# Low parts of all weight blocks on VectorE, fewer background steps in the feed-forward loops, and a later spectrum scaling

## The chip, the cores and the metric

The kernel runs on one core of a Trainium2 chip. The metric is the device time of one execution in microseconds (us); the median of three runs stands for a kernel. A profiled execution has a trace, whose span begins and ends with the first and last instruction that it records; its own time is a little longer than the span.

## The reference

Two layers of a diffusion backbone work on 256 latent tokens and 256 context tokens of 1024 features, in fp32. Each layer is a feed-forward, a token mixer, and a second feed-forward. Every sub-layer is modulated by shift, scale and gate vectors (adaLN) that come from `c` for the latent tokens and from `c_ctx` for the context, and is closed by a layer norm:

```python
def _ffn_sublayer(x, shift, scale, gate, w_in, w_out, g, b):
    a, u = jnp.split(_modulate(x, shift, scale) @ w_in, 2, axis=-1)   # 1024 -> 2 x 2816
    y = (jax.nn.silu(a) * u) @ w_out                                  # 2816 -> 1024
    return _post_ln(x, 0.5 * gate * y, g, b)                          # LN(alpha*x + ...)
...
for i in range(2):
    m  = silu(c) @ mod_w[i] + mod_b[i]        # 9 vectors of 1024 for the latent tokens
    mc = silu(c_ctx) @ mod_w[i] + mod_b[i]    # 9 for the context
    x  = _ffn_sublayer(x, m[0], m[1], m[2], ...);  xc = the same with mc
    h  = _modulate(x, m[3], m[4]);                 hc = the same with mc
    y  = even mixer (Fourier + Hyena long convolution) for i = 0
         odd mixer (two-way GLA + HGRN2 scans, the latent from the context's state) for i = 1
    x  = _post_ln(x, m[5] * y, ...)
    x  = _ffn_sublayer(x, m[6], m[7], m[8], ...)
```

The even mixer runs on both streams; in layer 1 the context is needed only as far as its scan states. The Hyena convolution multiplies spectra; its filters `k` come from a small network of the positions and are divided by the sum of their absolute values, `k / (sum |k| + 1e-6)`.

## The kernel before, in words

**Precision.** Every fp32 product is made of three (`mm3`, lines 463 to 465): an operand is cast to a high part (fp32r) and the rest is its low part; the products are high by high, high by low and low by high. Weights are split on the chip. `Stream` (line 39) holds the list of weight blocks (128 x 1024, 512 KB) in the order in which they are used. SP issues a block's load into one of three `raw` buffers; ScalarE casts it to `whi` (line 78); the low part `wlo` (or `lo`, for a block in spare buffers) is the difference of `raw` and `whi` (line 79), on GpSimd if the block's flag `pool` is set when it is queued, otherwise on VectorE. `whi` and `wlo` have three buffers each. `get()` hands a block out, splits the two after it and loads two further ones.

The flags come from the code that queues the blocks. In a feed-forward the input blocks alternate: the block for `pa` has its low part on VectorE, that for `pu` on GpSimd (`au == 1`). Of the output blocks most with an odd number go to GpSimd. In the mixers a table of numbers (`G0`) decides. In all, 164 low parts are made on GpSimd; 20 or 21 in each of the three feed-forward loops of both streams, 20 to 23 in each of their closes, the others in the mixers, their output products, the head and the last feed-forward.

**The feed-forward.** `ffn` (line 590) makes the hidden features. The first two of the 22 blocks of 128 come from a head in another layout; then 20 turns follow, f from 2 to 21. A turn has two units of 24 matmuls, into `pa` and `pu`. After each unit it advances a queue of background work, `bg`, by a step or two (`step`, line 166): one step after `pa`, two after `pu`. Then ScalarE takes the silu of `pa` (line 616), VectorE multiplies it by `pu` (line 617), ScalarE casts the result to `hh` (line 226) and GpSimd makes its low part (line 227). `hh` lies in 31 buffers of tag `s` that other stages use too, two blocks f per buffer and stream.

`ffn_close` (line 623) has two products of 22 units, of 12 matmuls each, `y <- whi, hh`: the first for the two latent tiles of tokens, the second for the two context tiles. In the first, `fill` advances `bg` by a step at every odd k; then `flush` runs what is left. In the second, the layer norms of the latent tiles are in `bg` and are advanced between the units. Layer norm works on VectorE for the most part (lines 331 to 353), with ScalarE, and GpSimd for the power (line 234).

**Background work.** `mod_vec` (line 238) makes an adaLN vector: for each of 8 blocks of `mod_w` (512 KB, loaded by SP into an `s` buffer) VectorE multiplies it by `c` and by `c_ctx` and sums along the row (line 243, two instructions `mt` of 128 x 1024 per block and step); then one step for the column (line 247), and for gates one with a transpose. In the first loop two generators advance together, so that a step has a part of each: `spectrum` (line 728) for the second Hyena filter, and the adaLN vectors 2 to 7 of layer 0. The second loop has five adaLN vectors, the third four.

`spectrum` takes the filter through: `lin` on TensorE, window and sums on VectorE and GpSimd, `norm1` (the sum of absolute values, in the bank `pn`), the reciprocal `rc` of it (lines 799, 800), diagonal blocks `eb` (line 803), then `scale()`: eight small matmuls `pr <- rc, eb` (line 758) that bring the reciprocal to all rows, and a copy by ScalarE to `rs`, by which the products `pk` are multiplied. A `yield` ends a step. The first filter's spectrum (`early`) runs in the head, whose order is a string written by hand.

**Order.** Each engine runs its instructions in the order in which the program issues them. There is no scheduler: where `step` is called fixes what stands ahead of what on VectorE, GpSimd, ScalarE, TensorE and in SP's queue of loads.

Of the kernel before, what the change touches and what calls it, by code (L numbers as in the profile page):

```python
# [9 lines left out]
F32 = mybir.dt.float32  # L10
# [4 lines left out]
ALU = mybir.AluOpType  # L15
# [23 lines left out]
class Stream:  # L39
# [26 lines left out]
    def split_to(self, i):  # L66
        while self.n_split <= min(i, len(self.units) - 1):
            j = self.n_split
            self.load_to(j + self.ahead_load)
            src, split, spare, pool = self.units[j]  # L70
            if split:
                w = self.raw.pop(j)
                if spare:
                    hi, lo = self.spare([P, 1024], F32R, "hi"), self.spare([P, 1024], F32R, "lo")
                else:
                    hi = self.pool.tile([P, 1024], F32R, tag="whi", name=f"whi{j}")
                    lo = self.pool.tile([P, 1024], F32R, tag="wlo", name=f"wlo{j}")
                self.nc.scalar.copy(hi, w)  # L78
                (self.nc.gpsimd if pool else self.nc.vector).tensor_tensor(lo, w, hi.bitcast(F32), op=ALU.subtract)  # L79
                self.split[j] = (hi, lo)  # L80
            self.n_split += 1

# [20 lines left out]
def g_(n, d):  # L103
    SEEN[n] = G0.get(n, d)
    return G.get(n, G0.get(n, d))
# [23 lines left out]
def kernel(ctx: ExitStack, tc: tile.TileContext, a, out, stop=None):  # L129
# [14 lines left out]
    def S(shape, dt=F32, name="s"):  # L144
        count[0] += 1
        return sp.tile(shape, dt, tag="s", name=f"{name}{count[0]}")

    def H(shape, dt=F32, name="h"):
        count[0] += 1
        return tp.tile(shape, dt, tag="h", name=f"{name}{count[0]}", bufs=5)  # L150
# [5 lines left out]
    def PS(name="ps"):  # L156
        count[0] += 1
        return ps.tile([P, 512], F32, tag="ps", name=f"{name}{count[0]}")
# [7 lines left out]
    def step(n=1):  # L166
        for _ in range(n):
            while bg:
                try:
                    next(bg[0])  # L170
                    break
                except StopIteration:
                    bg.pop(0)

    def flush():
        while bg:
            step()

    def run(*gens):
        for g in gens:  # L180
            for _ in g:
                pass
# [5 lines left out]
    def chain(*gens):  # L188
        for g in gens:
            yield from g  # L190
# [11 lines left out]
    def alternate(*gens):  # L202
        gens = list(gens)
        while gens:
            g = gens.pop(0)
            try:
                next(g)
                gens.append(g)
                yield
            except StopIteration:  # L210
                pass
# [13 lines left out]
    def split(dst_hi, dst_lo, src, lo_eng=None):  # L225
        act.copy(dst_hi, src)  # L226
        (lo_eng or dve).tensor_tensor(dst_lo, src, dst_hi.bitcast(F32), op=ALU.subtract)  # L227
# [62 lines left out]
    def load_ln(ln, l, n, gate, streams=2):  # L290

        ln.append(bcast(a["ln_g"][l, n:n + 1, :], "lng"))
        yield
        ln.append(bcast(a["ln_b"][l, n:n + 1, :], "lnb"))
        ln.append([])
        for s in range(streams):
            yield
            ln[2].append(bcast(gate_d[gate, s:s + 1, :], "gate"))
        yield
# [141 lines left out]
    def close(t, y, gate, g, b, ax, eps, nxt, late=False, fine=False):  # L441


        yield from post_ln(t, y, gate, g, b, ax, eps, fine)
        if nxt is None:
            return
        xn = {}
        yield from norm(t, xn)
        if "all" not in hT:
            new_hT()  # L450
        tr = zipped(to_hT(t, 0, xn[t], *nxt), to_hT(t, 1, xn[t], *nxt))
        if late:
            pend[t] = tr
        else:
            yield from tr
# [6 lines left out]
    def mm3(o, wh, wl, xh, xl, start, stop):  # L462
        pe.matmul(o, lhsT=wh, rhs=xh, start=start, stop=False)  # L463
        pe.matmul(o, lhsT=wh, rhs=xl, start=False, stop=False)  # L464
        pe.matmul(o, lhsT=wl, rhs=xh, start=False, stop=stop)  # L465

    def fm_unit(o, view=lambda x: x):

        hi, lo = ws.get()
        for k in range(KD):  # L470
            mm3(o, hi[:, P * k:P * k + P], lo[:, P * k:P * k + P], view(hT[k][:, 0, :]), view(hT[k][:, 1, :]), k == 0, k == KD - 1)
# [94 lines left out]
    def to_features(dst, pairs, h):  # L566

        yield
        pt = PS("pt")
        for f in range(2 * len(pairs)):  # L570
            pe.transpose(pt[:, P * f:P * f + P], h[:, P * f:P * f + P], ident)
        yield
        for n, b in enumerate(pairs):
            split(b[:, :, 0, dst], b[:, :, 1, dst], pt[:, 256 * n:256 * n + 256].rearrange("p (k t) -> p k t", k=2))
        yield
# [14 lines left out]
    def ffn(l, i, extra=(), head=None):  # L590
        hs = [{0: S([P, 2, 2, L], F32R, name="hh")} for s in range(2)]

        def done(t, y):
            h = H([P, 256], name="ht")
            act.activation(h, y[:, 0:256], AF.Silu)
            dve.tensor_tensor(h, h, y[:, 256:512], op=ALU.mult)
            return to_features(slice(P * (t % 2), P * (t % 2) + P), [hs[t // 2][0]], h)

        todo = (head or tm_head)(range(NT), done)
        bg.extend(extra)  # L600
        for f in range(2, KF):
            if f % 2 == 0:
                for s in range(2):
                    hs[s][f // 2] = S([P, 2, 2, L], F32R, name="hh")
            if f == 5 and stop == "head":
                return hs
            pa, pu = PS("pa"), PS("pu")
            fm_unit(pa)
            if todo:
                run(todo)  # L610
                todo = None
            step(1)
            fm_unit(pu)
            step(2)
            sa = H([P, T], name="sa")
            act.activation(sa, pa, AF.Silu)
            dve.tensor_tensor(sa, sa, pu, op=ALU.mult)  # L617
            for s in range(2):
                h = hs[s][f // 2][:, f % 2]
                split(h[:, 0], h[:, 1], sa[:, L * s:L * s + L], gp)  # L620
        return hs

    def ffn_close(l, i, hs, nxt):


        ln = []
        loads = load_ln(ln, l, 2 * i, GATE_ROW[l, 8 if i else 2])

        def lhs(k, t):
            h = hs[t // 2][k // 2][:, k % 2]  # L630
            c = slice(P * (t % 2), P * (t % 2) + P)
            return h[:, 0, c], h[:, 1, c]

        def fill(k):
            if k % 2:
                step(1)
            if k in range(10, 18, 2):
                next(loads)

        def closing(t, y, late=False):  # L640
            g, b, gates = ln
            return close(t, y, gates[t // 2], g, b, 2 * ALPHA, 4 * EPS, nxt, late, not late)

        y = tok_out(lhs, KF, (0, 1), fill)
        flush()
        hT.clear()
        k0 = key[0] = f"c{l}{i}"
        bg.append(alternate(closing(0, y[0]), closing(1, y[1])))

        def done(t, y):  # L650
            if t == 3:
                hs.clear()
            ws.split_spare(ws.pos + g_(f"{k0}a{t}", 2 * t - 3))
            if t == 3:
                flush()
            bg.append(closing(t, y, True))
            now.append(t)

        def fill(k):
            if now:  # L660
                step(g_(f"{k0}s3", 1))
            elif k >= KF - TAIL:
                step(g_(f"{k0}s2", 1))
            else:
                if k >= KF - TAIL - 3:
                    ws.split_spare(ws.pos + g_(f"{k0}b{KF - TAIL - k}", 1))
                step(g_(f"{k0}s1", 2) if k > g_(f"{k0}s0", 2) else 1)

        now = []
        tok_out(lhs, KF, (2, 3), fill, TAIL, done)  # L670


# [55 lines left out]
    def spectrum(o, hd, w3, win, cs, skip, T=None):  # L728
# [21 lines left out]
        def product(c, e):  # L750
            pk = PS("pk")
            mm3(pk, cs[:, c, 0, e], cs[:, c, 1, e], sd[e][0][:, c], sd[e][1][:, c], True, True)
            return pk
# [53 lines left out]
        if early:  # L807
            for n in todo[:2]:
                pks[n] = product(*n)
                yield  # L810
        rs = scale()
        yield
# [969 lines left out]
    hs = ffn(0, 0, [zipped(chain(spectrum(1, hd, con["w3"], con["win"], cs, lambda: con["skip"]), combine_first()), mods([(0, m) for m in range(2, 8)]))], head)  # L1782
# [14 lines left out]
    hs = ffn(0, 1, [mods([(0, 8)] + [(1, m) for m in range(4)])])  # L1797
# [4 lines left out]
    hs = ffn(1, 0, [mods([(1, m) for m in range(4, 8)])])  # L1802
# [113 lines left out]
```

## Time and profile before

| | us |
|---|---|
| median of 3 runs (1893.0 to 1899.78) | 1894.14 |
| profiled execution, its own time | 1893.39 |
| its span | 1891.6 |
| TensorE (PE) busy | 1761.0 |
| VectorE (DVE) busy | 1259.5 |
| ScalarE (ACT) busy | 724.8 |
| GpSimd (POOL) busy | 721.6 |

Windows of the span, from the trace: the head to 67 us, the loop of the first feed-forward to 321.4, its close to 449.8, the even mixer's products and transforms from 480.4 to 618, the second feed-forward's loop from 686.6 to 914.8, the third's from 1073.4 to 1298, the odd mixer from 1429.3 to 1648.3, the last feed-forward from 1713. Engines are named PE, PEld (weight loads of TensorE), DVE, ACT, POOL and SP in the rows; L79 is line 79. A tile's name is the one that the program gives it. "PEclk" is the clock of TensorE that was granted, as a share of 2.4 GHz.

### The profile page before, as it was taken

Reading aid. Unit: us, or ns where it says so; the run is one execution under the profiler, and the core shown is the slowest. Engines: PE = TensorE matmul, PEld = TensorE weight load, DVE = VectorE, ACT = ScalarE, POOL = GpSimd, SP = SyncE. Lnnn points to the kernel's source line nnn. Section 1 sums busy time; section 2 is a strip of 40 time slices with the busy share of each in tenths; the row PEclk is TensorE's granted clock in tenths of the full one; section 3 lists DMA queues with packets and bytes.
Section 4 is the critical chain, followed back from the end, with each engine's and each line's share of the span. In section 5 each row is a group of like instructions: output and inputs, shape, how many; then the busy total and the mean of one; then the engine's idle time right before and its main releaser. Section 6 shows DMA issues by size and latency. Waiting matters only on the chain. (4 is left out here: it accounts for less than half of the span.)

```text
span 1891.6 us, 22049 instructions
## 1 busy us (share of the span) xinstructions
PE 1761.0 (93%) x8236; PEld 1425.5 (75%) x8236; DVE 1259.5 (67%) x1674; ACT 724.8 (38%) x1070; POOL 721.6 (38%) x467
## 2 busy tenths in 40 slices
PE   6989999998987999999999999999988999879998
PEld 5767778876866778777887787788867778757887
DVE  6688887267599768885247688812377484676755
ACT  5422233344434342223334422323354463443443
POOL 2445434453356223333445233334454353341000
PEclk9989999999998999999999999999999999889999
DMA  8536654644313145553464455433644223335563
GB/s 317 214 132 240 227 189 166 238 167 150 112 45 123 65 164 202 208 203 130 154 233 177 150 213 199 162 110 138 232 166 145 83 91 90 134 131 201 206 215 137
DMA packets 91499, 314.91 MB, mean 166 GB/s; under 512 B 10848, under 2 KB 11584, under 8 KB 91392
## 3 DMA queue, kind: packets, MB, share of 16 engines
q1 hardware_dynamic: 85952, 297.09, 44.0%
q0 software_dynamic: 4576, 15.91, 2.6%
q8 instruction: 64, 1.05, 0.2%
q10 hardware_dynamic: 864, 0.51, 0.1%
q14 instruction: 43, 0.35, 0.1%
HBM read 308.18 MB, written 4.24 MB: 165 GB/s over the span
## 5 line engine op out<-in xcount | busy, mean ns | idle before, releaser
L79 DVE TENSOR_TENSOR wlo<-raw,whi 128x1024 fp32r<-128x1024 f32 x195 | 261.5, 1343 | 330.7 <-ACT whi L78 328.9
L79 POOL TENSOR_TENSOR wlo<-raw,whi 128x1024 fp32r<-128x1024 f32 x137 | 345.9, 2525 | 316.9 <-ACT whi L78 278.4
L78 ACT CAST whi<-raw 128x1024 fp32r<-128x1024 f32 x332 | 343.8, 1050 | 264.9 <-PE y L465 151.9
L243 DVE SCALAR_TENSOR_TENSOR mt<-mraw,cb 128x1024 bf16<-128x1024 f32 x256 | 395.8, 1599 | 11.2 <-DMA mraw<-in_mod_w_dram 8.3
L465 PE MATMUL pu<-hT,wlo 128*128 128x512 f32 x576 | 225.7, 392 | 4.7 <-DVE wlo L79 4.7
L463 PE MATMUL pu<-hT,whi 128*128 128x512 f32 x576 | 225.8, 392 | 0.0
L464 PE MATMUL pu<-hT,whi 128*128 128x512 f32 x576 | 225.4, 391 | 0.0
L227 POOL TENSOR_TENSOR hh<-sa,hh 128x256 fp32r<-128x256 f32 x120 | 87.1, 747 | 344.6 <-ACT hh L226 344.6
L465 PE MATMUL pa<-hT,wlo 128*128 128x512 f32 x480 | 191.3, 398 | 12.0 <-DVE wlo L79 12.0
L463 PE MATMUL pa<-hT,whi 128*128 128x512 f32 x480 | 191.5, 399 | 8.8 <-ACT whi L78 8.7
L464 PE MATMUL y<-wlo,hh 128*128 128x512 f32 x468 | 183.2, 391 | 6.8 <-DVE wlo L79 6.1
L464 PE MATMUL pa<-hT,whi 128*128 128x512 f32 x480 | 189.1, 394 | 0.0
L463 PE MATMUL y<-whi,hh 128*128 128x512 f32 x468 | 182.9, 391 | 0.2 <-ACT whi L78 0.2
L465 PE MATMUL y<-whi,hh 128*128 128x512 f32 x468 | 182.2, 389 | 0.0
L226 ACT CAST hh<-sa 128x256 fp32r<-128x256 f32 x120 | 42.8, 404 | 294.7 <-DVE sa L617 294.7
L465 PEld LDWEIGHTS pu<-hT,wlo 128*128 128x128 f32 x576 | 108.8, 189 | 28.3 <-DVE wlo L79 5.6
L463 PEld LDWEIGHTS pu<-hT,whi 128*128 128x128 f32 x576 | 109.0, 189 | 23.6 <-ACT hh L226 0.8
L464 PEld LDWEIGHTS pu<-hT,whi 128*128 128x128 f32 x576 | 108.9, 189 | 22.6
L465 PEld LDWEIGHTS pa<-hT,wlo 128*128 128x128 f32 x480 | 91.3, 190 | 39.7 <-DVE wlo L79 21.1
L463 PEld LDWEIGHTS pa<-hT,whi 128*128 128x128 f32 x480 | 91.4, 190 | 34.3 <-ACT whi L78 15.7
L464 PEld LDWEIGHTS y<-wlo,hh 128*128 128x128 f32 x468 | 87.8, 188 | 28.6 <-DVE wlo L79 8.4
L464 PEld LDWEIGHTS pa<-hT,whi 128*128 128x128 f32 x480 | 91.4, 190 | 18.7
(419 smaller groups left out, 3272.2 us busy)
## 6 DMA issues: line engine op xcount, KB each, us to landing
raw<-in_ffn_out_dram SPq DMA_DIRECT2D x154, 512.0 KB, 3.4
mraw<-in_mod_w_dram SPq DMA_DIRECT2D x144, 512.0 KB, 5.9
raw<-in_ffn_in_dram SPq DMA_DIRECT2D x120, 512.0 KB, 3.8
raw<-in_ffn_tm_dram SPq DMA_DIRECT2D x44, 512.0 KB, 3.3
raw<-in_od_fm_dram SPq DMA_DIRECT2D x17, 512.0 KB, 3.2
raw<-in_od_tm_dram SPq DMA_DIRECT2D x16, 512.0 KB, 3.3
raw<-in_ffn_head_dram SPq DMA_DIRECT2D x12, 512.0 KB, 4.4
raw<-in_ev_in_dram SPq DMA_DIRECT2D x12, 512.0 KB, 3.5
```

The source lines that it names most:

```text
L78: self.nc.scalar.copy(hi, w)
L79: (self.nc.gpsimd if pool else self.nc.vector).tensor_tensor(lo, w, hi.bitcast(F32), op=ALU.subtract)
L226: act.copy(dst_hi, src)
L227: (lo_eng or dve).tensor_tensor(dst_lo, src, dst_hi.bitcast(F32), op=ALU.subtract)
L243: dve.scalar_tensor_tensor(H([P, D], BF16, "mt"), w, 1.0, cb[s], op0=ALU.mult, op1=ALU.mult, accum_out=acc[:, s, b:b + 1])
L463: pe.matmul(o, lhsT=wh, rhs=xh, start=start, stop=False)
L464: pe.matmul(o, lhsT=wh, rhs=xl, start=False, stop=False)
L465: pe.matmul(o, lhsT=wl, rhs=xh, start=False, stop=stop)
```

## The change

Four edits. Line 79 makes every low part on VectorE, so that the flags are no longer read. A turn of a feed-forward loop has one or two steps after `pu` (one for an even f), not always two: 50 steps in a loop, not 60. In the close, at an odd k, the buffers of `hh` that the product has passed are given up one by one (`hs[0]` in the first product, `hs[1]` in the second), not all at the end. The `spectrum` of the second filter has three more yields between `eb` and `scale()`.

```diff
@@ split_to
                 self.nc.scalar.copy(hi, w)
-                (self.nc.gpsimd if pool else self.nc.vector).tensor_tensor(lo, w, hi.bitcast(F32), op=ALU.subtract)
+                self.nc.vector.tensor_tensor(lo, w, hi.bitcast(F32), op=ALU.subtract)
                 self.split[j] = (hi, lo)
@@ ffn
             step(1)
             fm_unit(pu)
-            step(2)
+            step(1 + f % 2)
             sa = H([P, T], name="sa")
@@ ffn_close, first product
         def fill(k):
             if k % 2:
+                hs[0].pop(k // 2)
                 step(1)
@@ ffn_close, second product
             else:
+                if k % 2:
+                    hs[1].pop(k // 2)
                 if k >= KF - TAIL - 3:
@@ spectrum
                 pks[n] = product(*n)
                 yield
+        else:
+            for _ in range(3):
+                yield
         rs = scale()
         yield
```

VectorE's queue in the first loop, before, around the reciprocal; `wlo` is a low part for a `pa` block, `gc` a column of adaLN, `sa` the gated features of a turn:

```order
L617 TENSOR_TENSOR sa_1071<-sa_1071,pu_981 128x512
L79 TENSOR_TENSOR wlo_1083<-raw_982,whi_1082 128x1024
L247 SCALAR_TENSOR_TENSOR gc_1127<-acc_849,modb 128x16
L799 TENSOR_SCALAR rc_1159<-pn_1110 128x128
L800 RECIPROCAL rc_1159<-rc_1159 128x128
L803 TENSOR_SCALAR eb_1162<-ones,ident 128x128 x4
L243 SCALAR_TENSOR_TENSOR mt_1170,acc_1167<-mraw_1059,cb_809 128x1024
L243 SCALAR_TENSOR_TENSOR mt_1172,acc_1167<-mraw_1059,cb_811 128x1024
L243 SCALAR_TENSOR_TENSOR mt_1183,acc_1167<-mraw_1065,cb_809 128x1024
L243 SCALAR_TENSOR_TENSOR mt_1185,acc_1167<-mraw_1065,cb_811 128x1024
L617 TENSOR_TENSOR sa_1187<-sa_1187,pu_1079 128x512
```

The same place after (lines of `spectrum` have moved by three):

```order
L617 TENSOR_TENSOR sa_1159<-sa_1159,pu_1061 128x512
L79 TENSOR_TENSOR wlo_1173<-raw_1062,whi_1172 128x1024
L802 TENSOR_SCALAR rc_1200<-pn_1140 128x128
L803 RECIPROCAL rc_1200<-rc_1200 128x128
L806 TENSOR_SCALAR eb_1203<-ones,ident 128x128 x4
L243 SCALAR_TENSOR_TENSOR mt_1211,acc_1208<-mraw_1098,cb_809 128x1024
L243 SCALAR_TENSOR_TENSOR mt_1213,acc_1208<-mraw_1098,cb_811 128x1024
L79 TENSOR_TENSOR wlo_1218<-raw_1104,whi_1217 128x1024
L243 SCALAR_TENSOR_TENSOR mt_1247,acc_1208<-mraw_1134,cb_809 128x1024
L243 SCALAR_TENSOR_TENSOR mt_1249,acc_1208<-mraw_1134,cb_811 128x1024
L617 TENSOR_TENSOR sa_1251<-sa_1251,pu_1169 128x512
```

A second low part, that of the `pu` block, now stands among the products of the turn.

ScalarE's queue before, around the copy of the scaling to `rs`:

```order
L616 ACTIVATE sa_1071<-pa_980 128x512
L226 CAST hh_978<-sa_1071 128x256
L226 CAST hh_979<-sa_1071 128x256
L78 CAST whi_1082<-raw_982 128x1024
L78 CAST whi_1131<-raw_1023 128x1024
L760 COPY rs_1179<-pr_1174 128x512
L616 ACTIVATE sa_1187<-pa_1078 128x512
```

And after:

```order
L616 ACTIVATE sa_1251<-pa_1168 128x512
L226 CAST hh_1166<-sa_1251 128x256
L226 CAST hh_1167<-sa_1251 128x256
L78 CAST whi_1262<-raw_1170 128x1024
L78 CAST whi_1298<-raw_1215 128x1024
L763 COPY rs_1337<-pr_1332 128x512
L616 ACTIVATE sa_1345<-pa_1258 128x512
```

Before, `rs` is copied ahead of the silu `sa_1187`, whose gating stands last in VectorE's piece before, so in the turn in which `rc` and `eb` are made. After, that turn's silu is `sa_1251`, and the copy comes ahead of the next one's, `sa_1345`: a turn later.

VectorE in the second product of the first close before, among the layer norms of two tiles (`z`, `x`), where `wlo` is a block's low part:

```order
L342 BN_AGGR mv_3141<-st_3036 128x2
L233 TENSOR_SCALAR rp_3144<-mv_3141 128x1
L79 TENSOR_TENSOR wlo_3150<-raw_3100,whi_3149 128x1024
L342 BN_AGGR mv_3165<-st_3057 128x2
L233 TENSOR_SCALAR rp_3168<-mv_3165 128x1
L347 SCALAR_TENSOR_TENSOR z_3035<-z_3035,mv_3141,lng_2807 128x1024
L347 SCALAR_TENSOR_TENSOR z_3056<-z_3056,mv_3165,lng_2807 128x1024
L353 SCALAR_TENSOR_TENSOR x_3171<-z_3035,rstd_3143,lnb_2845 128x1024
L79 TENSOR_TENSOR wlo_3197<-raw_3147,whi_3196 128x1024
```

And after:

```order
L342 BN_AGGR mv_3141<-st_3036 128x2
L233 TENSOR_SCALAR rp_3144<-mv_3141 128x1
L79 TENSOR_TENSOR wlo_3150<-raw_3100,whi_3149 128x1024
L342 BN_AGGR mv_3165<-st_3057 128x2
L233 TENSOR_SCALAR rp_3168<-mv_3165 128x1
L347 SCALAR_TENSOR_TENSOR z_3035<-z_3035,mv_3141,lng_2802 128x1024
L79 TENSOR_TENSOR wlo_3176<-raw_3121,whi_3175 128x1024
L347 SCALAR_TENSOR_TENSOR z_3056<-z_3056,mv_3165,lng_2802 128x1024
L353 SCALAR_TENSOR_TENSOR x_3171<-z_3035,rstd_3143,lnb_2844 128x1024
L79 TENSOR_TENSOR wlo_3197<-raw_3147,whi_3196 128x1024
```

The low part `wlo_3176`, which was on GpSimd, stands between the two `z` of line 347.

## Rows read from the trace of the kernel before

**Rows 1.** Busy time, share of the span and instructions of each engine:
```profile
PE 1761.0 (93%) x8236; PEld 1425.5 (75%) x8236; DVE 1259.5 (67%) x1674; ACT 724.8 (38%) x1070; POOL 721.6 (38%) x467
```
**Rows 2.** Windows: us, busy (count) of PE, PEld, DVE, ACT, POOL; PEclk, DMA share, GB/s:
```profile
67.00:321.40 254.40, 236.63 (x1027) 188.19 (x1025) 209.67 (x259) 71.06 (x113) 109.99 (x77) 0.97 0.54 197
119.50:129.50 10.00, 5.77 (x18) 4.91 (x19) 9.90 (x17) 1.40 (x4) 2.49 (x1) 0.50 0.74 259
686.60:914.80 228.20, 221.88 (x967) 179.60 (x966) 163.68 (x206) 65.22 (x104) 79.79 (x60) 1.00 0.51 188
1073.40:1298.00 224.60, 220.37 (x964) 179.73 (x963) 138.98 (x173) 65.82 (x103) 76.99 (x59) 1.00 0.48 174
1232.70:1298.00 65.30, 65.30 (x289) 54.05 (x288) 11.97 (x12) 19.27 (x30) 22.99 (x18) 1.00 0.30 104
480.40:618.00 137.60, 121.12 (x561) 98.81 (x561) 116.90 (x149) 57.27 (x91) 71.47 (x39) 0.94 0.28 94
...
1624.50:1641.60 17.10, 15.48 (x63) 13.24 (x64) 7.96 (x14) 2.42 (x4) 0.77 (x1) 0.50 0.28 92
```
**Rows 3.** Groups by line: busy us, mean ns of one, idle before and its releaser:
```profile
L79 DVE TENSOR_TENSOR wlo<-raw,whi 128x1024 fp32r<-128x1024 f32 x195 | 261.5, 1343 | 330.7 <-ACT whi L78 328.9
L79 POOL TENSOR_TENSOR wlo<-raw,whi 128x1024 fp32r<-128x1024 f32 x137 | 345.9, 2525 | 316.9 <-ACT whi L78 278.4
...
L243 DVE SCALAR_TENSOR_TENSOR mt<-mraw,cb 128x1024 bf16<-128x1024 f32 x256 | 395.8, 1599 | 11.2 <-DMA mraw<-in_mod_w_dram 8.3
L465 PE MATMUL pu<-hT,wlo 128*128 128x512 f32 x576 | 225.7, 392 | 4.7 <-DVE wlo L79 4.7
...
L227 POOL TENSOR_TENSOR hh<-sa,hh 128x256 fp32r<-128x256 f32 x120 | 87.1, 747 | 344.6 <-ACT hh L226 344.6
...
L465 PE MATMUL pa<-hT,wlo 128*128 128x512 f32 x480 | 191.3, 398 | 12.0 <-DVE wlo L79 12.0
...
L464 PE MATMUL y<-wlo,hh 128*128 128x512 f32 x468 | 183.2, 391 | 6.8 <-DVE wlo L79 6.1
```
**Rows 4.** Single lines: count, then duration ns min/median/max, first and last start us:
```profile
L243 DVE SCALAR_TENSOR_TENSOR mt<-mraw,cb x256: 1207/1216/3421, 79.6 to 1788.0; 128x1024 bf16<-128x1024 f32 x128
...
L79 DVE TENSOR_TENSOR wlo<-raw,whi x195: 1193/1226/3409, 60.2 to 1872.7; 128x1024 fp32r<-128x1024 f32 x195
...
L79 POOL TENSOR_TENSOR lo<-raw,hi x27: 2340/2418/3381, 22.8 to 1692.6; 128x1024 fp32r<-128x1024 f32 x27
...
L353 DVE SCALAR_TENSOR_TENSOR x<-z,rstd,lnb x9: 1272/3402/3427, 403.9 to 1430.6; 128x1024 f32<-128x1024 f32 x9
```
**Rows 5.** Timeline, one turn of the second loop: start us, us, instruction, [idle before]:
```profile
739.14 1.32 DVE L79 TENSOR_TENSOR wlo<-raw,whi 128x1024 fp32r<-128x1024 f32 x1 [1.73 <-ACT whi L78]
740.20 2.52 POOL L79 TENSOR_TENSOR wlo<-raw,whi 128x1024 fp32r<-128x1024 f32 x1 [0.81 <-POOL hh L227]
740.38 3.42 DVE L243 SCALAR_TENSOR_TENSOR mt<-mraw,cb 128x1024 bf16<-128x1024 f32 x1
...
743.73 1.22 DVE L243 SCALAR_TENSOR_TENSOR mt<-mraw,cb 128x1024 bf16<-128x1024 f32 x1
...
749.46 0.68 DVE L617 TENSOR_TENSOR sa<-sa,pu 128x512 f32<-128x512 f32 x1
...
751.87 1.30 DVE L79 TENSOR_TENSOR wlo<-raw,whi 128x1024 fp32r<-128x1024 f32 x1 [1.74 <-ACT whi L78]
```
**Rows 6.** Timeline, TensorE at the scaling in the first loop:
```profile
123.73 2.08 PE L758 MATMUL pr<-rc,eb 128*128 128x128 f32 x8 [7.59 <-DVE eb L803]
```
**Rows 7.** Timeline, three waits of TensorE in and after the mixers:
```profile
1438.50 1.75 PE L411 MATMUL ptr<-ident,xn 128*128 128x128 f32 x7 [6.15 <-ACT xn L398]
...
1615.83 6.44 DVE L1419 SCALAR_TENSOR_TENSOR OH<-OH,rr,gn 128x128 f32<-128x128 f32 x8
...
1626.12 0.77 PE L1351 MATMUL po<-vg,am 128*128 128x128 f32 x2 [4.45 <-DVE am L1345]
...
1738.41 0.79 PE L464 MATMUL ya<-wlo,hT 128*128 128x512 f32 x1 [3.21 <-DVE wlo L79]
```

## What I expect of the change, and why

> **What bounds the kernel now.** I began with the busy shares [rows 1]: TensorE works for 1761.0 of 1891.6 us, so all that an edit can give back is TensorE's idle time, 130.6 us, and the time in which its clock is low. VectorE (1259.5) and GpSimd (721.6) bound nothing on average. Next I cut the span into windows by stage [rows 2]. A piece of the last feed-forward without a waiting matmul gives the free pitch: 288 matmuls in 65.30 us, 0.2267 each, so a unit of 24 takes 5.44 us and a loop of 20 turns (40 units) 217.6 us. The three feed-forward loops take 254.4, 228.2 and 224.6 us; what stands above 217.6 is 36.8, 10.6 and 7.0, and of the first 36.8 some 10 belong to the extra matmuls of the filter spectrum (1027 against 967). In the even mixer VectorE is busy for 116.9 of 137.6 us; it is the one stage where that engine is close to being the limit.
>
> Then the groups by cost [rows 3] show who holds TensorE up: in the loops the matmuls of `pa` and `pu` waited 12.0 + 4.7 us for low parts, in the second products `y` waited 6.1 us for them. All of these were made on VectorE. Why VectorE is late is in the spread of single durations [rows 4]: the product of an adaLN step (line 243) takes 1.216 us as median and up to 3.421; a low part on VectorE 1.226 and up to 3.409; line 353 has 1.272 at best and 3.402 as median. One turn of a loop shows the cause [rows 5]: GpSimd's low part runs from 740.20 to 742.72, and the VectorE product issued at 740.38 ends only at 743.80. By itself it takes 1.22; it stood still until GpSimd was done. So the 2.4 us low parts on GpSimd are paid for on VectorE.
>
> The Trainium skill, "SBUF — State Buffer", section "Who interferes with whom", says that a VectorE instruction with two SBUF operands and a GpSimd instruction that reads SBUF share a port under an exclusive lock, where the loser stands still and isn't merely slowed. The trace agrees (1.22 became 3.42 behind a GpSimd instruction of 2.52); by that rule the stretch goes with the subtractions, and of the large groups on GpSimd only the 0.747 us instructions of line 227 [rows 3] remain to cause some.
>
> **What the edits do to VectorE's load.** 164 subtractions (137 + 27) leave GpSimd [rows 3, 4]. On VectorE they are worth 164 x 1.226 = 201 us. What comes back: line 243, 256 x (1.599 - 1.216) = 98; its own low parts, 195 x (1.343 - 1.226) = 23; line 353, up to 9 x 2.1 = 19; smaller groups add some. So VectorE's busy total grows by 30 to 60 us, to about 1300 (69%), while its single instructions become 1.2 us long throughout. GpSimd falls by 137 x 2.525 + 27 x 2.418 = 411 to about 310 us.
>
> **The loops.** A turn now takes VectorE from 739.14 to 751.87 = 12.73 us, more than TensorE's two units (10.88), so TensorE waits [rows 5]. In it are a wait of 1.73 for the next high part, one low part, a first product of 3.35 start to start, five more at 1.146 (743.73 to 749.46), and the gating product of 0.68. After: wait 1.73, two low parts at 1.2, the gating product, and one or two adaLN steps between them, so four or six products of 1.15 (a step is two; three steps before, two or three now). That is 1.73 + 2.4 + 0.6 + 4.6 or 6.9 = 9.3 or 11.6, 10.5 as mean against 10.88. The odd turns run over by 0.7 and the even ones give it back; low parts are asked for two units ahead. So TensorE should hardly wait. The second loop then gains most of its 10.6: I take 7. The third, with 7.0 above the pitch, I take at 5. Bounds: 0 and 17.6 for the two.
>
> In the first loop one wait stands alone: the scaling matmuls `pr` wait 7.59 us for `eb` at 123.73 [rows 6], and the clock in 119.5 to 129.5 is granted at 0.50 [rows 2], the lower level (1.2 GHz), which costs 10 x 0.5 = 5 more. With three more yields the matmuls stand behind the next turn's `pu` unit, some 11 us after `eb` is issued, and VectorE has no longer an 11 us stretch ahead of it without a break, so the whole 12.7 should go. The rest of the first loop: PE idle there is 254.4 - 236.63 = 17.8, less 7.6 for `pr` leaves 10.2; the mean clock of 0.97 means about 7.6 lost, less 5 leaves 2.6. Of these 12.8 I take 11, because spectrum work still falls on VectorE between low parts. First loop: 24. Bounds: 0 (if the `eb` wait only moves) and 26.
>
> **The closes.** The second products gain the 6.1 us of `y` [rows 3]: the low parts that waited lose their stretch. Against that, 20 to 23 low parts per close now lie in VectorE's order among layer-norm work, and where that work exceeds TensorE's 12 x 0.2267 = 2.72 us per unit, TensorE must live from the two units split ahead (5.44 us). I take the 6.1 as won. The first loop has 50 steps now, not 60, and its six vectors need 48 for their blocks and some for columns and gates; six blocks are left for the first product of its close: per block 2 x 1.15 us on VectorE, which has little to do there, and a 512 KB load on SP's queue among the product's own. The product streams 0.524 MB per 2.72 us, 193 GB/s; six blocks in 22 units add 53. The 246 stay under the 259 that [rows 2] shows in a window at a share of 0.74, so the loads should fit; I charge 1, with bounds 0 and 4. The tiles given back one by one only let such loads start earlier; that is in the same charge. Net 5; bounds -12 and 6, the lower from 3 closes x 3.8 us, if an excess of half a microsecond in each of seven units per close isn't covered by the two units ahead.
>
> **The other places.** Low parts of mixers and heads: 40 or so of the 164 (20 to 21 in each loop, 20 to 23 in each close). Three waits there hang on a stretched instruction [rows 7]. At 1615.83 eight small products take 6.44 us beside a GpSimd low part, `am` is late, and TensorE waits 4.45 at 1626.12: all of it. `ya` at 1738.41 waits 3.21 for a low part: all of it. `ptr` at 1438.50 waits 6.15 at the end of a chain that has line 353 at 1430.6 in it: 3.4 - 1.27 = 2.1. Together 10. After 1626 the clock is at 0.50 for 17.1 us [rows 2], a loss of 8.5 behind that 4.45 wait; I count half, 4, since I can't tell that this wait alone brought it down. For the even mixer I charge 2: five low parts more on VectorE are 5 x 1.22 = 6.1 of loss in the stage where it is busiest, against up to five stretches of 2.2 that go, 11.
>
> The Trainium skill, "Perfetto Trace Analysis", section "Optimizing Scalar/DVE Operations", advises to move work away from VectorE, to ScalarE or even GpSimd, where VectorE is saturated, with the warning that the shared port may undo it. By the advice the even mixer should lose the 6.1; by the warning it should gain. The trace has both sides there, and only the run can tell.
>
> **The sum.** 24 + 7 + 5 + 5 + 10 + 4 - 2 = 53. The profiled execution took 1893.4 us (1.8 outside its span): 1893.4 - 53 = 1840. The median of the runs is 0.7 above it, which is less than the rounding here.
>
> **Rivals.**
> B, the loops alone gain. In closes and mixers the in-order VectorE queue loses with the added low parts what its shorter instructions win. Gains: 24 + 7 + 5 = 36, less 3 x 3 in the closes and nothing in the mixers: 27, so 1866. For it: `y` already waits for VectorE, not GpSimd, low parts. Against it: those very waits are stretched.
> C, slower: VectorE's queue becomes the bound outside the loops. A low part that GpSimd made beside everything else now stands behind whatever VectorE has ahead of it. If each of the 40 in mixers and heads is exposed for its 1.22 (49 us), the closes lose 3 x 3.8 = 11.4, and the loops gain only the `pr` stall and half the rest (12.7 + 12 = 25), the result is 1893.4 + 49 + 11.4 - 25 = 1929; half of the exposure gives 1904. It decides once VectorE is busy in a mixer for nearly all of its window; the even mixer, at 85%, is the only one close. Against it: TensorE, ScalarE and the chains leave gaps in the odd mixer's VectorE work.
> D, the subtraction isn't what stretches. If the stretch belonged to other GpSimd work (line 227, 120 x 0.747), the load would grow by 201 and only the `pr` stall would go: 1893.4 - 12.7 = 1880, or worse. Against it: 3.42 fits 2.52 + 1.22 less the overlap, and line 227 is too short for that.
>
> **Chances.** Forecast 0.68 (own range 1822 to 1858), B 0.18 (1858 to 1872), D 0.07, C 0.07. Runs of this kernel can't tell less than about 0.5%, 9.5 us, from no change: faster means under 1884.7, which the forecast, B and half of D give, 0.89; same 0.05, from the rest of D and the weakest of C; slower 0.06. The range 1820 to 1870 holds the forecast's own and most of B.
>
> **What would show it.** Right: line 243's median and mean both near 1.22 with a maximum near 2.0; VectorE near 1300 us busy, GpSimd near 310; no `pr` wait above 1 us and clock 1.0 around 120 us; second and third loop at 218 to 222 us; `pa` and `pu` waits for low parts under 5 us in all; the `am` wait gone. Wrong: `y` waiting over 10 us for `wlo` in the second products (B), waits for `wlo`, `lo` or mixer tiles of VectorE in the even mixer beyond those of before with that window above 140 us (C), or line 243 still reaching 3.4 (D).

## The result, and the profile after

The changed kernel takes 1831.66 us (median of 4 runs, 1826.96 to 1833.66) against 1895.55 (4 runs): a ratio of 0.9657, 95% interval 0.9629 to 0.9685. The forecast was 1840, range 1820 to 1870, so the direction and the size were right. Some of the terms behind them were not: the scaling edit won nothing, the loops gained more than the most that was allowed for the first, and the clock's 4 us didn't come, as the runs below show.

Busy time of each engine after, in the columns of [rows 1]:

```profile
PE 1746.5 (95%) x8236; PEld 1425.9 (78%) x8236; DVE 1277.3 (70%) x1838; ACT 725.4 (40%) x1070; POOL 307.5 (17%) x303
```

VectorE took over 164 instructions and is busy only 18 us longer, and GpSimd lost 414 us. The reason stands in the spread of single durations (count, then ns min/median/max), which answer to [rows 4], and in the groups that answer to [rows 3]:

```profile
L243 DVE SCALAR_TENSOR_TENSOR mt<-mraw,cb x256: 1208/1217/2312, 77.1 to 1728.4; 128x1024 bf16<-128x1024 f32 x128
...
L353 DVE SCALAR_TENSOR_TENSOR x<-z,rstd,lnb x9: 1278/1282/2396, 378.0 to 1385.2; 128x1024 f32<-128x1024 f32 x9
```

```profile
L79 DVE TENSOR_TENSOR wlo<-raw,whi 128x1024 fp32r<-128x1024 f32 x332 | 420.5, 1270 | 319.4 <-ACT whi L78 319.0
...
L243 DVE SCALAR_TENSOR_TENSOR mt<-mraw,cb 128x1024 bf16<-128x1024 f32 x256 | 309.8, 1251 | 2.1 <-DMA mraw<-in_mod_w_dram 2.1
...
L464 PE MATMUL y<-wlo,hh 128*128 128x512 f32 x468 | 183.5, 392 | 3.0 <-DVE wlo L79 3.0
```

The adaLN product's mean went from 1.599 to 1.251 us, its longest from 3.421 to 2.312; line 353's median from 3.402 to 1.282. No wait of a matmul of `pa` is left.

The windows after, columns of [rows 2]: the first loop, its close, the even mixer, the second and third loop, the odd mixer, each from the same matmul as before:

```profile
67.40:293.10 225.70, 225.70 (x1027) 184.97 (x1026) 181.46 (x252) 71.42 (x114) 56.04 (x54) 1.00 0.58 208
293.10:420.80 127.70, 124.18 (x546) 100.13 (x545) 94.58 (x124) 56.41 (x65) 10.72 (x12) 1.00 0.66 222
453.90:594.00 140.10, 123.05 (x561) 100.48 (x560) 122.00 (x154) 56.95 (x91) 58.59 (x34) 0.93 0.29 96
661.30:879.60 218.30, 218.30 (x966) 180.51 (x966) 154.50 (x226) 65.82 (x104) 28.35 (x40) 1.00 0.54 195
1038.40:1256.40 218.00, 218.00 (x965) 180.35 (x964) 137.33 (x193) 66.36 (x103) 27.84 (x39) 1.00 0.50 178
1384.70:1595.90 211.20, 201.23 (x1088) 169.50 (x1087) 134.07 (x218) 103.50 (x174) 53.06 (x39) 0.95 0.35 112
```

In all three loops TensorE's busy time is the window: it never waits, and the clock is at 1.00. They give 28.7, 9.9 and 6.6 us (45.2 of the 59.7 by which the span fell). The closes give 4.3, the odd mixer 7.7, what follows it 7.3 (its output product 2.7, the head and body of the last feed-forward 1.3 and 3.3), the head of the second feed-forward 1.5. The even mixer loses 2.6 and the stretches ahead of the mixers and loops some 4.

Where the time went, by stage, in us between the same matmuls of each kernel (e1 to e4 are the first four experiments):

| stage | before | after | e1 low parts | e2 scaling | e3 steps | e4 low parts + steps |
|---|---|---|---|---|---|---|
| first loop | 254.4 | 225.7 | 236.4 | 252.1 | 235.6 | 225.7 |
| its close | 128.4 | 127.7 | 127.0 | 128.2 | 132.4 | 128.0 |
| even mixer | 137.5 | 140.1 | 139.9 | 138.4 | 138.2 | 140.1 |
| second loop | 228.2 | 218.3 | 218.3 | 228.2 | 218.3 | 218.3 |
| third loop | 224.6 | 218.0 | 218.0 | 224.6 | 218.0 | 218.0 |
| third close | 131.3 | 128.3 | 127.8 | 131.1 | 131.5 | 127.8 |
| odd mixer | 219.0 | 211.2 | 209.8 | 216.6 | 218.3 | 211.0 |
| median of runs | 1894.7 | 1831.7 | 1840.3 | 1895.3 | 1867.0 | 1830.7 |

(The median in the column before is that of the runs beside e1 to e4; the one in the column after is that of the result above.)

### The profile page after: what moved, and what is told of

Its sections match the earlier page's. It is cut to its first block, busy times and chain, and to the rows that moved or that the text cites. A ratio compares the mean times of both kernels' runs of the same rounds, so it can differ in the third digit from the quotient of the medians.

```text
span 1831.9 us, 22048 instructions
## 1 busy us (share of the span) xinstructions
PE 1746.5 (95%) x8236; PEld 1425.9 (78%) x8236; DVE 1277.3 (70%) x1838; ACT 725.4 (40%) x1070; POOL 307.5 (17%) x303
## 5 line engine op out<-in xcount | busy, mean ns | idle before, releaser
L79 DVE TENSOR_TENSOR wlo<-raw,whi 128x1024 fp32r<-128x1024 f32 x332 | 420.5, 1270 | 319.4 <-ACT whi L78 319.0
L243 DVE SCALAR_TENSOR_TENSOR mt<-mraw,cb 128x1024 bf16<-128x1024 f32 x256 | 309.8, 1251 | 2.1 <-DMA mraw<-in_mod_w_dram 2.1
L463 PE MATMUL pa<-hT,whi 128*128 128x512 f32 x480 | 187.6, 391 | 0.0
L465 PE MATMUL pa<-hT,wlo 128*128 128x512 f32 x480 | 186.8, 389 | 0.0
L464 PE MATMUL pa<-hT,whi 128*128 128x512 f32 x480 | 186.8, 389 | 0.0
L234 POOL TENSOR_TENSOR rstd<-rp,mhalf 128x1 f32<-128x1 f32 x42 | 35.4, 847 | 483.9 <-DVE rp L233 481.0
```

The source lines that it names most:

```text
L79: self.nc.vector.tensor_tensor(lo, w, hi.bitcast(F32), op=ALU.subtract)
L234: gp.tensor_tensor(dst, t, mhalf.to_broadcast([P, n]), op=ALU.pow)
L243: dve.scalar_tensor_tensor(H([P, D], BF16, "mt"), w, 1.0, cb[s], op0=ALU.mult, op1=ALU.mult, accum_out=acc[:, s, b:b + 1])
```

## The experiments

**One edit at a time.** The first two edits each by itself, on the kernel before.

e1, the low parts alone:

```diff
-                (self.nc.gpsimd if pool else self.nc.vector).tensor_tensor(lo, w, hi.bitcast(F32), op=ALU.subtract)
+                self.nc.vector.tensor_tensor(lo, w, hi.bitcast(F32), op=ALU.subtract)
```

Expected:

> The kernel before with the one edit of line 79: every low part on VectorE, three steps per turn, scaling where it was. Theory: a turn of a feed-forward loop is VectorE work against TensorE's 10.88 us; without GpSimd's subtraction the turn of three steps takes 11.6 us instead of 12.73, still too long, so about 60% of what the loops won beside the scaling (32 us) is here, 20 us; mixers, closes and tails win their 19 less 5 for the even mixer: about 1860 us, second loop near 222. Rival 1, the fewer steps alone won the loops: about 1880, second loop at 228. Rival 2, the low parts alone won them: about 1848, second loop at 218. The scaling wait stays above 5 us in all of them.

Measured: 1840.26 us, ratio 0.9706 (0.9685 to 0.9727). The theory of 60% fell. In the second and third loop TensorE no longer waits at all:

```profile
670.20:888.50 218.30, 218.30 (x966) 180.51 (x966) 153.06 (x226) 66.77 (x104) 28.33 (x40) 1.00 0.54 195
1047.30:1265.30 218.00, 218.00 (x965) 180.36 (x964) 136.03 (x193) 66.85 (x103) 27.84 (x39) 1.00 0.49 178
```

So rival 2 had it right for these two loops. In the first loop, where `spectrum` adds work to VectorE, only 18.0 of the 28.7 us came, and `pr` still waits, though 3.9 us and not the more than 5 that I expected (waits of TensorE: total, times, longest):

```profile
PE pr L758 <- DVE eb L803: 3.9, 1, 3.9
```

e2, the three yields alone:

```diff
+        else:
+            for _ in range(3):
+                yield
         rs = scale()
```

> The kernel before with only the three yields ahead of the scaling. Theory: the wait of 7.59 us for eb and the 10 us at half clock go, 12.7 us: about 1881 to 1882, first loop 242 us. Rival: the wait only moves to the next thing that VectorE is late with, a gain under 4 us: 1890 to 1895.

Measured: 1895.32 us (10 runs), ratio 0.9996 (0.9983 to 1.0009): nothing. The wait of 7.59 us for `eb` is gone, yet the first loop is only 2.3 us shorter, because others have come. Timeline of TensorE in e2 (start, us, instruction, idle before it):

```profile
118.47 0.50 PE L463 MATMUL pa<-hT,whi 128*128 128x512 f32 x1 [2.79 <-ACT whi L78]
119.79 0.79 PE L465 MATMUL pa<-hT,wlo 128*128 128x512 f32 x1 [0.39 <-DVE wlo L79]
...
160.05 0.79 PE L463 MATMUL pa<-hT,whi 128*128 128x512 f32 x1 [2.23 <-ACT whi L78]
...
199.17 0.50 PE L463 MATMUL pa<-hT,whi 128*128 128x512 f32 x1 [2.80 <-ACT whi L78]
```

and the loop's window, whose mean clock is 0.97 as before:

```profile
66.80:318.90 252.10, 236.73 (x1027) 187.44 (x1026) 211.03 (x259) 71.14 (x114) 110.09 (x77) 0.97 0.55 198
```

The rows name ScalarE's high part `whi`, but ScalarE had itself been held up by VectorE. In its queue the casts of `hh` stand ahead of that of `whi`, and they waited 5.13 us for VectorE's gated features `sa` (timeline of ScalarE in e2):

```profile
116.76 0.71 ACT L226 CAST hh<-sa 128x256 fp32r<-128x256 f32 x2 [5.13 <-DVE sa L617]
117.38 1.99 ACT L78 CAST whi<-raw 128x1024 fp32r<-128x1024 f32 x2
```

VectorE has the same work in the loop (211.0 us, 209.7 before). Moving the matmul that waits for it only changed which matmul waits. The theory fell, the rival that the wait only moves held.

e3, the fewer steps with the buffers given up one by one, low parts on GpSimd as before:

```diff
-            step(2)
+            step(1 + f % 2)
...
             if k % 2:
+                hs[0].pop(k // 2)
                 step(1)
...
+                if k % 2:
+                    hs[1].pop(k // 2)
```

> The kernel before with only the fewer steps (one or two after pu) and the buffers given up one by one; low parts on GpSimd as before. Theory: turns of 12.73 and 10.4 us alternate, 11.6 as mean, so some 60% of 32 us: about 1875, second loop near 222, with line 243 still reaching 3.4 us. Rival 1, the steps alone won the loops: 1862, second loop 218. Rival 2, the low parts alone won them: 1890 to 1895, second loop 228.

Measured: 1867.04 us, ratio 0.9846 (0.9821 to 0.9871). The second and third loop lose their waits here too, with GpSimd's low parts still in them (81 to 85 us of GpSimd) and line 243 still reaching 3.45 us:

```profile
676.70:895.10 218.40, 218.40 (x967) 180.59 (x968) 169.88 (x206) 66.12 (x104) 84.66 (x60) 1.00 0.55 197
1052.80:1270.80 218.00, 218.00 (x965) 180.40 (x964) 143.40 (x173) 66.45 (x103) 81.03 (x59) 1.00 0.51 180
```

So in the second and third loop either edit is enough, and my "some 60% each" was wrong for both; rival 1 held for these loops. e3 doesn't tell the fewer steps from the buffers given up one by one. What e3 gains it partly returns: the first close takes 4.0 us longer. Six adaLN blocks have moved there, beside GpSimd's low parts; after, with the same blocks and no such low parts, it is 0.7 shorter.

e4, the changed kernel without the three yields (the diff of e2, reversed):

> The changed kernel without the three yields, scaling in the turn of eb. Theory: the wait of pr comes back with 5 to 7 us and with it the half clock: 1843 to 1845, first loop 237 us. Rival, the wait was due to the stretch of VectorE's instructions (a column of 2.31 us lay in it) and doesn't come back: 1831 to 1835.

Measured: 1830.68 us, ratio 0.9658 (0.9637 to 0.9680), first loop 225.7 us, as after. `pr` follows without a wait:

```profile
125.39 0.83 PE L761 MATMUL pr<-rc,eb 128*128 128x128 f32 x6
```

The scaling edit is worth nothing alone and nothing beside the others. The rival held: the wait came from VectorE's lateness, and goes with it. (In e1 it was 3.9 us, in e3 2.8.)

**What GpSimd's subtraction does to VectorE.** Three kernels add one instruction per turn to e1 in the second and third loop, on a tile of its own that nobody else reads (and that GpSimd fills once ahead of the loop). e5 adds a GpSimd subtraction, e6 a GpSimd fill, e9 a VectorE subtraction:

```diff
+        dm = S([P, 1024], name="dm") if l + i == 1 else None
...
             fm_unit(pu)
+            if l + i == 1:
+                gp.tensor_tensor(dm, dm, dm, op=ALU.subtract)   # e5
+                gp.memset(dm, 0.0)                              # e6, in its place
+                dve.tensor_tensor(dm, dm, dm, op=ALU.subtract)  # e9, in its place
             step(2)
```

> e1 (low parts on VectorE, three steps per turn) with one GpSimd subtraction of 128x1024 added per turn in the second and third loop; it reads and writes a tile of its own and nothing waits for it. Theory: GpSimd's subtraction itself holds VectorE up: line 243 reaches 3.4 us again in these loops, and they rise from 218 to at least the 228 and 224.6 us of before, up to 245 (VectorE has one low part per turn more than before): 1857 to 1890. Rival: what counted was only VectorE's own load and its order; the loops stay at 218: 1838 to 1842.

Measured: 1870.28 us (1865.95 to 1875.46), ratio 0.9861 (0.9833 to 0.9889). The loops rise by 17.3 and 13.9 us over those of e1, to more than before:

```profile
668.70:904.30 235.60, 225.67 (x967) 181.82 (x967) 179.74 (x226) 65.21 (x104) 81.96 (x59) 0.99 0.51 181
1064.40:1296.30 231.90, 223.04 (x965) 180.69 (x964) 157.73 (x193) 65.81 (x103) 81.50 (x58) 0.99 0.46 166
```

GpSimd, and below it VectorE, in one turn of e5 (timeline: start, us, instruction):

```profile
722.24 2.88 POOL L618 TENSOR_TENSOR dm<-dm 128x1024 f32<-128x1024 f32 x1
```

```profile
723.28 2.91 DVE L243 SCALAR_TENSOR_TENSOR mt<-mraw,cb 128x1024 bf16<-128x1024 f32 x1
726.12 1.22 DVE L243 SCALAR_TENSOR_TENSOR mt<-mraw,cb 128x1024 bf16<-128x1024 f32 x1
```

The product issued at 723.28 ends at 726.19, 1.07 us after GpSimd's instruction (725.12): it did its own work only then. No data passes between the two. That GpSimd's subtraction holds VectorE up is shown with that, in place and price. The longest is 2.9 us here and not the 3.4 that I expected: in every turn that holds a product up like this, VectorE comes to it 1.04 to 1.06 us into GpSimd's instruction.

> As the run with the added subtraction, but the added GpSimd instruction only fills the tile with zero: it writes 128x1024 and reads nothing. If a GpSimd instruction holds VectorE up only where it reads SBUF: the loops stay at 218 us, 1838 to 1842. If every GpSimd access does so for as long as it runs: line 243 is stretched by the duration of the fill and the loops rise, 1845 or more.

Measured: 1839.97 us, ratio 0.9699 (0.9676 to 0.9722), loops of 218.3 and 218.0 us: as e1. A fill on GpSimd, and VectorE beside it:

```profile
707.14 0.97 POOL L618 MEMSET dm<- 128x1024 f32 x1
```

```profile
706.98 1.30 DVE L79 TENSOR_TENSOR wlo<-raw,whi 128x1024 fp32r<-128x1024 f32 x1 [1.73 <-ACT whi L78]
```

The low part has the fill beside it for all of its 0.97 us and takes 1.30, what it takes after the same wait where GpSimd is idle (1.30 at 718.80 after). By itself that says little, since VectorE had begun first: in e5 the low part at 722.05, 0.19 us ahead of the subtraction, takes 1.31 too. But the fill isn't held either: it takes 0.94 to 0.98 us in all 40 places, while e5's subtraction takes 1.91 us in two places and 2.87 to 2.89 in the 38 where a low part has begun just ahead of it. And once in e5, e6 and e9 each, at the fill ahead of the third loop, GpSimd begins first and a low part follows 0.53 us later. It takes 1.21 us; here the rows of e9:

```profile
1053.02 0.95 POOL L603 MEMSET dm<- 128x1024 f32 x1
```

```profile
1053.55 1.21 DVE L79 TENSOR_TENSOR wlo<-raw,whi 128x1024 fp32r<-128x1024 f32 x1
```

So this GpSimd instruction, which only writes, doesn't hold VectorE up, and the loops agree. The tile is the same as in e5, so it wasn't the tile that cost e5 its time. That the fill is harmless because it reads nothing, and not for another difference from a subtraction, is not shown.

> e1 (low parts on VectorE, three steps per turn) with one more subtraction of 128x1024 per turn on VectorE itself in the second and third loop, into a tile of its own; nothing waits for it. Theory: what counts is VectorE's time per turn against TensorE's 10.88 us, whatever fills it. In e1 it is 1.73 + 2.45 + 0.6 and 80 products of 1.145 us over 15.7 turns, 10.6 in the mean; with 1.15 more 11.76: 0.88 us over in 15.7 and 12.7 turns, less some 3 us of lead: second loop near 229, third near 226, total 1857 to 1862. Rival: only GpSimd's hold on single instructions matters, VectorE has room for 1.15 us: loops under 220, total 1838 to 1842.

Measured: 1859.40 us, ratio 0.9809 (0.9792 to 0.9825). The loops:

```profile
670.60:899.60 229.00, 222.09 (x967) 179.64 (x967) 175.47 (x246) 65.16 (x104) 28.27 (x40) 1.00 0.51 186
1058.50:1283.80 225.30, 220.56 (x964) 179.67 (x963) 158.47 (x213) 65.79 (x103) 27.80 (x39) 1.00 0.48 174
```

229.0 and 225.3 where 229 and 226 were expected. So the budget is right: TensorE doesn't wait when VectorE's turn stays under TensorE's 10.88 us in the mean, whether the time is spent on work or on standing still behind GpSimd. The same count, as an estimate, says why either edit was enough. In the second loop's steps the instructions of lines 243 and 79 exceed 1.22 us by 31 us in all before, 2.0 per turn, and by 38 in e3, 2.1 per turn. Before, 80 products in 15.7 turns make 1.73 + 1.22 + 0.6 + 5.8 + 2.0 = 11.4 us a turn; in e3 the same steps spread over 18.8 turns, 1.73 + 1.22 + 0.6 + 4.9 + 2.1 = 10.5.

**Where low parts on VectorE cost something.** e7 puts the even mixer's flagged input blocks back on GpSimd, e8 those of the odd mixer and its output:

```diff
-                self.nc.vector.tensor_tensor(lo, w, hi.bitcast(F32), op=ALU.subtract)
+                (self.nc.gpsimd if pool == 2 else self.nc.vector).tensor_tensor(lo, w, hi.bitcast(F32), op=ALU.subtract)
...
+            ws.add(a["ev_in"][f], True, False, 2 * g_(f"qei{f}", 0))   # e7; e8: the same for od_fm, od_tm, od_out
```

> The changed kernel with the input blocks of the even mixer that were on GpSimd put back there (four or five low parts). Theory: the low part that stands ahead of z in VectorE's queue near 546 us is exposed there; pz waits 2.5 us instead of 4.85, the even mixer goes from 140.1 to about 137.5 us, the total to about 1829. Rival: the difference of 2.6 us is of the clock or of the order elsewhere; the mixer stays at 140 and the total at 1831.

Measured: 1828.28 us, ratio 0.9638 (0.9622 to 0.9654), even mixer 138.1 us. Below stand TensorE's wait for `z` after, VectorE's queue ahead of it after, and the same wait in e7:

```profile
550.99 0.80 PE L464 MATMUL pz<-z,dft 128*128 128x512 f32 x1 [4.86 <-DVE z L227]
```

```profile
545.75 2.29 DVE L79 TENSOR_TENSOR wlo<-raw,whi 128x1024 fp32r<-128x1024 f32 x1
547.97 1.64 DVE L888 SCALAR_TENSOR_TENSOR cv<-pu,cw,cv 128x256 f32<-128x256 f32 x4
549.53 1.41 DVE L227 TENSOR_TENSOR z<-r,z 128x512 fp32r<-128x512 f32 x1
```

```profile
545.91 0.51 PE L464 MATMUL pz<-z,dft 128*128 128x512 f32 x1 [2.50 <-DVE z L227]
```

One low part of 2.29 us stands ahead of `z` in VectorE's queue, and the wait is longer by 2.36. That is the mechanism of rival C, at one place; its sign, the even mixer above 140 us, showed after (140.1).

> The changed kernel with the low parts of the odd mixer and its output that were on GpSimd put back there (18 or so). Theory: the mixer's 7.7 and the output's 2.7 us come from these instructions: 1840 to 1843, with the am wait of 4 us back. Rival: they come from what stands before the mixer (phase, clock): 1830 to 1834.

Measured: 1836.97 us, ratio 0.9685 (0.9669 to 0.9702), between the two forecasts. The odd mixer takes 217.1 us against 211.2 after, but its mean clock is 0.93 against 0.95; TensorE's idle time in it is 12.1 against 10.0 us, and the wait for `am` 2.8 against 1.9. The output product takes as long as after. Of the odd mixer's 7.7 us 7.0 are idle time of TensorE that went (17.0 before, 10.0 after); these low parts bring some 2 of it back, and 3.8 more in matmuls at the lower mean clock (busy 205.0 us against 201.2). `ptr` waits 4.4 as after, so its 1.8 us don't come from them. One build alone says little of that clock, but all together do: the four profiles with these low parts on GpSimd (before, e2, e3, e8) take 216.6 to 219.0 us in the mixer, the nine with them on VectorE 204.2 to 211.2. That the output's 2.7 us come from the blocks of the last feed-forward, split meanwhile and on VectorE in e8 too, is argued and wasn't run.

**A better version.** e7 was run again beside the changed kernel on one chip.

> The changed kernel once more, beside the next one on the same chip: 1827 to 1834, with the odd mixer between 205 and 211 us as its clock falls.

> The changed kernel with the even mixer's flagged input blocks on GpSimd, once more: theory, 2 to 3.5 us faster than the changed kernel beside it; rival, within 1 us of it.

Measured: 1831.06 (1831.0 to 1831.55) and 1824.92 us (1822.49 to 1830.25); ratios to before 0.9662 (0.9647 to 0.9676) and 0.9633 (0.9613 to 0.9652). The medians favour e7 both times, by 3.4 and 6.1 us, the second more than either forecast, yet the intervals overlap. The two profiles of this pair put only 1.1 us into the even mixer (139.2 against 140.3), where `pz` again waits 2.5 us and not 4.8, but a wait of `pu` has grown from 2.6 to 4.1; 5.1 us are in the odd mixer (205.5 against 210.6), whose code is the same. What e7's edit can be shown to be worth is the 1 to 2 us of the even mixer.

## Why the prediction was right, and where its steps were not

**The mechanism held.** GpSimd's subtraction stretches VectorE's instructions; with it gone, 164 more of them cost VectorE 18 us in all (30 to 60 were forecast, so the stretch that went was undersized; GpSimd, put at 310, has 307.5). e5 shows the cause with nothing but the hold added, and e6 leaves out the tile as a rival. The Trainium skill, "SBUF — State Buffer", section "Who interferes with whom", says of a two-operand VectorE instruction and a GpSimd instruction that reads SBUF that the loser stands still. 723.28 to 726.19 us in e5 agrees.

**The first loop: the gain came, by other parts.** I took 12.7 us for the scaling stall and 11 for the rest, 24 with an upper bound of 26; measured 28.7, above the bound. The step that failed is "With three more yields ... so the whole 12.7 should go". e2 gave 2.3, e4 against after gives 0. The row that named `eb` as the releaser was right, the inference wasn't: VectorE was behind its turn by a few microseconds, and whatever TensorE wanted next would have waited. What the loop won came from the other two edits, 18.0 and 18.8 alone, 28.7 together; that the forecast's 12.7 came at all was luck for this term. My share for the extra matmuls was also too high (10; the window after, without a wait, leaves 225.7 - 217.6 = 8.1).

The prediction's list of waits also left out a row, which e2 shows to be VectorE's lateness handed on by ScalarE (waits of TensorE before):

```profile
PE pa L463 <- ACT whi L78: 8.7, 13, 1.7
```

All 13 stand behind casts of `hh` that waited for VectorE's `sa`.

**The second and third loop: undersized.** 7 and 5 were taken, 9.9 and 6.6 measured, all that stood above a loop without waits. I counted three steps as six products of 1.15 us in every turn, 11.6 us for e1. But of the 47 steps of the second loop only 40 are blocks, so the mean is, as an estimate, 1.73 + 2.45 + 0.6 + 80 x 1.145 / 15.7 = 10.6, already under 10.88. A turn in the second loop after, VectorE:

```profile
707.94 1.30 DVE L79 TENSOR_TENSOR wlo<-raw,whi 128x1024 fp32r<-128x1024 f32 x1 [1.73 <-ACT whi L78]
...
711.79 1.23 DVE L79 TENSOR_TENSOR wlo<-raw,whi 128x1024 fp32r<-128x1024 f32 x1 [0.26 <-ACT whi L78]
...
716.38 0.69 DVE L617 TENSOR_TENSOR sa<-sa,pu 128x512 f32<-128x512 f32 x1 [1.08 <-issue]
718.80 1.30 DVE L79 TENSOR_TENSOR wlo<-raw,whi 128x1024 fp32r<-128x1024 f32 x1 [1.74 <-ACT whi L78]
```

It is 718.80 - 707.94 = 10.86 long, TensorE's pace, and VectorE now waits (0.26, 1.08) where TensorE did [rows 5]. I also put the 4.7 us that `pu` waits into the loops; the two waits (2.16 and 2.56 before) lie in the even mixer, which uses the same tile name, and 4.8 of them are still there.

**The closes** gave 4.3 where 5 was taken; `y` waits 3.0 us for `wlo` and not 6.1. The charge of 1 for the six blocks was fair: the first close gained 0.7 with them, 1.3 without (e1).

**The other places.** `am`: 4.45 became 1.9, where I had said that it would be gone; `ya`: 3.21 became 1.6, in three waits; `ptr` after line 353: 6.15 became 4.35. That is 6.0 of the 10 taken. The 4 us of clock didn't come: the stretch behind `am` (1571 to 1590 us after) has a mean clock of 0.58. All stages from the odd mixer on gave 15.0 together, near the 14 taken, but not by those rows alone, and the odd mixer's share moves with its clock from build to build: that this sum came so close is in part luck.

**The even mixer** lost 2.6 where 2 was charged, by the exposed low part that e7 shows. The Trainium skill, "Perfetto Trace Analysis", section "Optimizing Scalar/DVE Operations", says that moving work off a saturated VectorE, even to GpSimd, may make sense, and that the shared port may undo it. In this one stage, where VectorE is busy for 122.0 of 140.1 us, e7 does so, with 2.0 and 1.1 us won. The 2.4 us lost between first close and even mixer I'd have put down to low parts as well; but e2 and e3, without them on VectorE, lose 2.8 and 2.2 there, and e4, with them, none: the mean clock of that stretch is 0.94 before, 0.90 after and in e2 and e3, and 1.00 in e4. What brought it down is not shown.

**The rivals.** D is excluded by line 243's new durations and e5. C is real at one place and worth 2 us there; the 49 us that it put on the forty low parts of mixers and heads didn't come. B fell: the closes and the odd side gained.

## What to carry to other kernels

When an in-order engine is late, the row with the wait names whom it hit, not what to move: compare the engine's work per turn with the pace of the one that waits, count the steps that really are long, and take time out of the turn; two edits that each get below the pace don't add up. A GpSimd subtraction like this one isn't beside VectorE's two-operand work but ahead of it: 2.4 us there were dearer here than 1.2 us in VectorE's own queue, save in one stage, the even mixer, where that queue is nearly full.

## What the runs showed of the hardware that I had not expected

A GpSimd fill of 128x1024 (0.96 us) runs beside VectorE without a trace (a low part begun 0.53 us into it takes 1.21 us), while a subtraction of the same shape stops it (2.91 us for 1.22). The hold goes both ways: that subtraction itself takes 1.91 us in two places of e5 and 2.87 to 2.89 in the other 38, which all start 0.15 to 0.2 us after a low part on VectorE.

The granted clock varies between builds in stages whose instructions there are the same: the odd mixer took 204.2 to 205.5 us at a mean clock of 0.97 to 0.98 in e5, e6 and e11, and 209.8 to 211.2 at 0.95 in e1, e4, e7, e9, e10 and after. Most of the difference lies behind `am`. In e5 and e11 the matmul that needs it doesn't wait; but in e6 it waits 1.5 us, as in e1, and the clock still stays up. Windows from that matmul to the mixer's end, in the columns of [rows 2], for e1 and then e6:

```profile
1581.50:1602.90 21.40, 21.38 (x104) 18.05 (x104) 9.05 (x16) 4.92 (x10) 2.63 (x4) 0.68 0.47 166
1580.50:1597.30 16.80, 16.79 (x105) 13.95 (x105) 8.74 (x16) 4.84 (x10) 2.63 (x4) 0.90 0.66 201
```

Why the same wait brings the clock down in one build and not in the other stays open. Differences of up to 7 us between two builds in that stage say nothing by themselves of an edit elsewhere.
